# A hybrid decoder block on one core: the mean inside the third product, gates as pairs of 64-row matmuls, one block's residual fetched later, and another end

## The chip, the core and the metric

The kernel runs on one core of one Trainium2 chip. The metric is the device time of one execution in microseconds. The work is on five engines with queues of their own: TensorE (PE, with its weight loads PEld), VectorE (DVE), ScalarE (ACT), GpSimd (POOL) and SyncE (SP), which issues most DMAs.

## What is computed

One decoder layer over 2048 positions of 1024 channels, in fp32. The reference, cut:

```python
h = rms_norm(x, norm1_g)
z = h @ w_in                       # 2*1024 + 3*512 columns
lru_x, lru_gate, sc_b, sc_c, sc_x = split(z)
lru_x = causal_dwconv(lru_x, lru_conv_w) + lru_conv_b
r = sigmoid(blockdiag16x64(lru_x, wa) + ba)     # 16 heads of 64 channels
i = sigmoid(blockdiag16x64(lru_x, wx) + bx)
log_a = -8 * r * softplus(-lam)
hs = scan(a = exp(log_a), b = sqrt(1 - exp(2*log_a)) * i * lru_x)
y = concat(hs * gelu(lru_gate), sc_b * causal_dwconv(sc_c * sc_x))
x = x + y @ w_out
h = rms_norm(x, norm2_g)
gate, up = split(causal_dwconv(h @ w_up, ffn_conv_w))
x = x + (gelu(gate) * up) @ w_down
out = rms_norm(x, final_g)
```

## The kernel before

Channels lie on the 128 partitions, positions in the free dimension. The sequence goes in two halves of T = 1024 positions, each in two blocks of NB = 512. Every fp32 product is made of three matmuls in fp32r: each operand is split into a high and a low part (`split`: ACT makes the high part, DVE the low one), and high x high, high x low and low x high are summed in PSUM.

Six phases follow each other: the input phase of the first half (7 to 345 us), its output sweep o0 (to 461), the input phase of the second half (to 789), sweep o1 (to 910), then up and down of the first half and of the second. A sweep multiplies by w_out or w_down in seven passes over 512 x 512 blocks and adds the residual (`sweeps`, `TAKEN`). The residual blocks "11", "12", "22" and "21" are fetched at steps of the sweep that a table gives.

In the input phase (`in_phase`) one product of 48 matmuls (8 blocks of channels x 3 x 2 blocks of positions) makes 128 columns of z. Products 0 and 8 come first, each step as x arrives. Then comes the mean: the squares of x are summed on ACT and DVE into ss_a, split into rh_a and rl_a (`mean_split`), and four matmuls with a matrix of 1/D sum them over the partitions into ms_a; ACT and DVE make the inverse root of it (`inv_rms`), by which each product is scaled when it leaves PSUM. In the first half product 1 stands before the four matmuls. Then twelve units run in the order L0 L1 S0 L2 L3 S1 L4 L5 L6 L7 S2 S3. An L unit c is a group of 128 recurrent channels, two heads: xl (product c, scaled), cv (the convolution: one step on ACT, three on DVE), xch and xcl (its high and low parts), the gates, sigmoids r and i, then a, m (in the tile of cv), a scan and the product with the gelu of the gate g (product 8 + c).

The gates of a unit are one group of 12 matmuls, three for each of r and i and each block, with the 128 x 128 weights of r and of i (two heads on the diagonal, zeros beside it) in gw, the split of a raw tile that is loaded behind the weights of product 8 + c. "Gate group c" below is the group of unit c. On PE it stands behind the product of the next unit and ahead of product 8 + c + 1.

PE, SP and POOL run in the order in which the program issues their instructions; for ACT and DVE a scheduler sets the order, with priorities (HP 120, HW 90, HE 30). Raw weights have two buffers (wr), PSUM has eight banks of 128 x 512, and a product or a gate tile of both blocks takes two.

`decay_rates` computes 8 * softplus(-lam) from the parameters with some thirty operations of 128 x 8. `sum_step` makes sums of w_out blocks in DRAM (so_d), a copy on SP's queue and an adding DMA on POOL's after each product, once the list `ready` allows it. At the end, `down1_done` squares the last block of the output (sq_last), splits the square and adds it to the last mean, and `finish_block` scales eight blocks and sends them out.

Of the kernel before, what the change touches and what calls it, by code (L numbers as in the profile page):

```python
# [7 lines left out]
F32 = mybir.dt.float32  # L8
# [4 lines left out]
P = 128  # L13
# [13 lines left out]
HE = 30  # L27
WARM = 11
NOUT = NLRU + NSC
NI = NFF // 2  # L30
# [38 lines left out]
def block_kernel(  # L69
# [28 lines left out]
    nc8 = cp.tile([P, NLRU], F32, name="nc8")  # L98
    xl_halo = cp.tile([P, NLRU, 3], F32, name="xl_halo")
    h_last = cp.tile([P, NLRU], F32, name="h_last")  # L100
    p_halo = cp.tile([P, NSC, 2], F32, name="p_halo")
# [47 lines left out]

    def decay_rates():  # L150
        z = cp.tile([P, NLRU], F32, name="dz")
        t = cp.tile([P, NLRU], F32, name="dt")
        e = cp.tile([P, NLRU], F32, name="de")
        s2 = cp.tile([P, NLRU], F32, name="ds2")
        lam = prm[:, O_LAM : O_LAM + NLRU]
        nc.vector.tensor_scalar(z, lam, -1.0, None, ALU.mult)
        nc.vector.tensor_tensor(z, z, lam, ALU.max)
        nc.scalar.activation(t, z, AF.Tanh, scale=1.0 / 16.0)
        nc.vector.tensor_scalar(e, t, 1.0, None, ALU.add)
        nc.vector.reciprocal(e, e)  # L160
        nc.vector.tensor_scalar(t, t, -1.0, 1.0, ALU.mult, ALU.add)
        nc.vector.tensor_tensor(e, e, t, ALU.mult)
        for _ in range(3):
            nc.vector.tensor_tensor(e, e, e, ALU.mult)
        nc.vector.tensor_scalar(t, e, 2.0, None, ALU.add)
        nc.vector.reciprocal(t, t)
        nc.vector.tensor_tensor(t, t, e, ALU.mult)
        nc.vector.tensor_tensor(s2, t, t, ALU.mult)
        nc.vector.tensor_scalar(e, s2, 1.0 / 21.0, None, ALU.mult)
        for k in range(9, 0, -1):  # L170
            nc.vector.scalar_tensor_tensor(e, e, 1.0 / (2 * k + 1), s2, ALU.add, ALU.mult)
        nc.vector.scalar_tensor_tensor(e, e, 1.0, t, ALU.add, ALU.mult)
        nc.vector.tensor_scalar(t, lam, -1.0, 0.0, ALU.mult, ALU.max)
        nc.vector.scalar_tensor_tensor(t, e, 2.0, t, ALU.mult, ALU.add)
        nc.vector.tensor_scalar(c8, t, 8.0, None, ALU.mult)
        nc.vector.tensor_scalar(nc8, t, -8.0, None, ALU.mult)
# [25 lines left out]

    gate_raw = {}

    def load_parts(src, name, parts, gate=None):
# [5 lines left out]
        for i in range(parts):  # L211
            ks = slice(i * n, (i + 1) * n)
            nc.sync.dma_start(raw[:, ks], src[:, ks])
            with tc.high_priority(offset=HW):
                split(hi[:, ks], lo[:, ks], raw[:, ks])
            if gate is not None and i == 0:
                gate_raw[gate] = tile_[:, 4, : 2 * P]
                nc.sync.dma_start(gate_raw[gate], w_gate[gate])
            yield hi, lo
# [17 lines left out]

    def product(ps, wts, acts):
        n = len(acts)
        for k in range(n):  # L240
            product_step(ps, wcol(wts, k), acts[k], k == 0, k == n - 1)

# [16 lines left out]
    def inv_rms(acc, name, parts=None):  # L259
# [3 lines left out]
        for i, x in enumerate(terms):  # L263
            for b, p in enumerate(pss):
                nc.tensor.matmul(p, ones_r, r32(x[:, blk(b)]), start=i == 0, stop=i == len(terms) - 1)
        with tc.high_priority(offset=HP):
# [46 lines left out]
    def gate_weights(c, half):  # L313
        raw = gate_raw[c]
        gw = flat(act(f"gw{half}_{c}"))
        hi, lo = gw[:, 0 : 2 * P], gw[:, 2 * P : 4 * P]
        with tc.high_priority(offset=HW):
            split(hi, lo, raw)
        return hi, lo

    def lru_gates(c, half, xc, gw):
        pss = []
        for g, name in enumerate("ri"):
            ps = pst2(f"z{name}{half}_{c}")
            product_step(ps, wcol(gw, g), xc, True, True)
            pss.append(ps)
        return pss

    def lru_scan(c, half, cv, g, ps_r, ps_i):
        n = f"{half}_{c}"  # L330
        r, i, a = (flat(act(f"{x}{n}")) for x in "ria")
        with tc.high_priority(offset=HP):
            for dst, ps, o in ((r, ps_r, O_BA), (i, ps_i, O_BX)):
                for b, p in enumerate(ps):
                    nc.scalar.activation(dst[:, blk(b)], p, AF.Sigmoid, bias=col(o + c))
        nc.vector.tensor_tensor(i, i, cv, ALU.mult)
# [23 lines left out]

    def in_product(o, half, acts):
        ps = pst2(f"zin{half}_{o}")
        product(ps, load_weights(w_in[o], f"in{half}_{o}", o - NLRU if NLRU <= o < 2 * NLRU else None), acts)
        if len(ready) > half:
# [47 lines left out]
    def in_phase(half, acts, acc, between):  # L412
# [18 lines left out]
        parts = mean_split(acc, f"a{half}")  # L431
        gw = gate_weights(0, half)
        ps_2 = in_product(1, half, acts) if half == 0 else None
        rs = inv_rms(acc, f"a{half}", parts)
        nc.gpsimd.tensor_copy(ones[:, 0:1], rs[:, 0:1])
        ready.append(True)
        xc, cv = lru_conv(0, half, pss[0], rs)
        if half == 0:
            decay_rates()
        cur = (xc, cv, lru_gate(0, half, pss[1], rs))  # L440
        ps_n = None
        for n, (kind, c) in enumerate(UNITS):
            nxt = UNITS[n + 1] if n + 1 < len(UNITS) else None
            if kind == "L":
# [5 lines left out]
                ps_g = in_product(NLRU + nxt[1], half, acts) if n == 0 else None  # L450
                if n > 0:
                    gw = gate_weights(c, half)
                gates = lru_gates(c, half, xc, gw)
                if nxt[0] == "L":
# [226 lines left out]
    def sweeps(half, wsrc, fsrc, ni, name, residual, done, beside, tail=0):  # L681
        res = {}
        fetch = {}
        for key, at in (("11", ((0, 1), (0, 2))), ("12", ((1, 0), (1, 0))), ("22", ((1, 1), (1, 2))), ("21", ((6, 1), (6, 1)))):
            for p, a in enumerate(at):
                fetch.setdefault(a, []).append((key, p))
        step = 0
        for s, (wo, fo, on_x) in enumerate(SWEEPS):
# [40 lines left out]
            for m in range(4):  # L729
                for h in held:  # L730
                    mm((m,), *h)
                for key, sign, final in TAKEN[s]:
                    r = res[key][m // 2][:, m % 2, :]
                    with tc.high_priority(offset=HP if last else HE):
                        nc.vector.tensor_tensor(r, r, ps[m], ALU.add if sign > 0 else ALU.subtract)
# [160 lines left out]
    def finish_block(t, rs):  # L896
        for key in ("12", "22") if t else ("11", "21"):
            mh = PLACE[key][0]
            for p, r in enumerate(kept[key]):
                for m in range(2):  # L900
                    scaled(r[:, m, :], 4 * mh + 2 * p + m, rs)
                c = 4 * mh + 2 * p
                o = T + t * NB
                defer(4, yT[c : c + 2, :, o : o + NB].rearrange("m p c -> p m c"), r)

    def down1_done(key, m, r):
# [3 lines left out]
        with tc.high_priority(offset=HP if key == "21" else 0):  # L910
            if key == "21" and m == 3:
                sq = flat(tmp("sq_last"))[:, :NB]
                nc.scalar.activation(sq, r[:, 1, :], AF.Square)
                terms.extend(mean_split(sq, "l2"))
                return
# [33 lines left out]
def _arrange(i):  # L949
# [6 lines left out]
    out["w_in"] = f["w_in"][0].reshape(KC, P, 28, P).transpose(2, 1, 0, 3).reshape(28, P, D)  # L956
    wg = np.zeros((NLRU, P, 2, P), x.dtype)
    for g, name in enumerate(("lru_wa", "lru_wx")):
        w = f[name][0].reshape(NLRU, 2, 64, 64)
        wg[:, 0:64, g, 0:64] = w[:, 0]  # L960
        wg[:, 64:128, g, 64:128] = w[:, 1]
    out["w_gate"] = wg.reshape(NLRU, P, 2 * P)
    w = f["w_out"][0].reshape(NOUT, P, D)
# [42 lines left out]
```

## Time and profile before

| | us |
|---|---|
| median of 3 runs (2302.47 to 2308.16) | 2305.39 |
| profiled execution | 2304.75 |
| its span in the trace | 2302.9 |
| PE busy | 2272.7 |
| DVE busy | 1723.8 |
| ACT busy | 1136.0 |
| POOL busy | 141.4 |

The time of the profiled execution is 1.85 us longer than its span, which ends with the last instruction's effect. A matmul's record is longer than the interval to the next one's start, since matmuls follow each other in the array before the first is through; so two starts are compared where the price of one is wanted.

### The profile page before, as it was taken

How to read it: one execution, taken by the hardware profiler on the slowest of the kernel's cores; microseconds unless marked ns; L12 is line 12 of the kernel's file. 1: busy time of each engine (PE TensorE's matmuls, PEld its weight loads, DVE VectorE, ACT ScalarE, POOL GpSimd, SP SyncE). 2: the span in 40 equal slices, each digit the busy share in tenths (PEclk: the TensorE clock that was granted, in tenths of full speed). 3: DMA queues.
4: the chain of work that ended last, by engine and by line, in shares of the span. 5: the costliest groups of instructions: out<-in, count | busy, mean ns of one | idle time of the engine just before them, and what ended most of it. 6: DMA issues, size and time to landing. Idle time of an engine off the chain costs nothing.

```text
span 2302.9 us, 26017 instructions
## 1 busy us (share of the span) xinstructions
PE 2272.7 (99%) x9984; PEld 1875.2 (81%) x9984; DVE 1723.8 (75%) x1910; ACT 1136.0 (49%) x1242; POOL 141.4 (6%) x232
## 2 busy tenths in 40 slices
PE   8999999999999999999999999999999999999997
PEld 7788887888888878888888888888888888888885
DVE  7656668767666898888787877578888888886556
ACT  5553645545547345554444444455544444443443
POOL 0001000000010000111010100000010000000000
PEclk9999999999999999999999999999999999999999
DMA  5356257766755767223232348576223232348754
GB/s 182 106 141 162 80 183 243 271 177 147 195 156 143 235 246 248 102 92 114 92 114 92 114 155 289 204 242 216 87 92 115 92 119 88 122 169 324 256 186 181
DMA packets 145597, 378.28 MB, mean 164 GB/s; under 512 B 13824, under 2 KB 17024, under 8 KB 144896
## 3 DMA queue, kind: packets, MB, share of 16 engines
q1 hardware_dynamic: 135680, 357.74, 44.8%
q0 software_dynamic: 9792, 18.88, 5.2%
q8 instruction: 78, 1.28, 0.2%
q14 instruction: 47, 0.39, 0.0%
HBM read 289.53 MB, written 124.78 MB: 180 GB/s over the span
## 4 chain that ended last, share of the span: by engine, by line
PE 94%; DVE 3%; DMA 1%; ACT 1%; issue 1%; SPq 0%; DVEq 0%; ACTq 0%
PE zin_b L234 25%; PE zx L581 23%; PE zc L581 11%; PE dx L700 11%; PE dy L700 8%; PE za L581 6%; PE ox L700 5%; PE oy L700 3%; PE zr_b L234 1%; PE zi_b L234 1%; DMA x<-in_xT 1%; DMA wr_d<-sd_d_S 0%; DVE x2r L879 0%; DVE cv L294 0%; DVE fl_o L196 0%
## 5 line engine op out<-in xcount | busy, mean ns | idle before, releaser
L234 PE MATMUL zin_b<-xh,wh_in 128*128 128x512 f32 x896 | 277.2, 390 | 4.8 <-DVE ss_a L270 2.6
L234 PE MATMUL zin_b<-xl,wh_in 128*128 128x512 f32 x896 | 277.0, 390 | 0.1
L234 PE MATMUL zin_b<-xh,wl_in 128*128 128x512 f32 x896 | 276.3, 390 | 0.0
L234 PEld LDWEIGHTS zin_b<-xh,wh_in 128*128 128x128 f32 x896 | 168.5, 188 | 40.9 <-DVE ss_a L270 3.5
L234 PEld LDWEIGHTS zin_b<-xl,wh_in 128*128 128x128 f32 x896 | 168.5, 188 | 36.4 <-DVE xl L402 1.7
L234 PEld LDWEIGHTS zin_b<-xh,wl_in 128*128 128x128 f32 x896 | 168.5, 188 | 35.0
L196 DVE TENSOR_TENSOR fl_d<-wr_d,fh_d 128x1024 fp32r<-128x1024 f32 x84 | 102.8, 1223 | 104.5 <-ACT fh_d L195 102.2
L195 ACT ACTIVATE fh_d<-wr_d 128x1024 fp32r<-128x1024 f32 x84 | 89.1, 1061 | 176.7 <-PE dy L700 79.7
L196 DVE TENSOR_TENSOR wla_up<-wr_up,wha_up 128x1024 fp32r<-128x1024 f32 x48 | 58.8, 1226 | 139.0 <-ACT wha_up L195 139.0
L700 PE MATMUL dx<-fl_d,wh_d 128*128 128x512 f32 x384 | 149.5, 389 | 0.8 <-DVE fl_d L196 0.8
L700 PE MATMUL dx<-fh_d,wl_d 128*128 128x512 f32 x384 | 149.4, 389 | 0.0
L700 PE MATMUL dx<-fh_d,wh_d 128*128 128x512 f32 x384 | 149.4, 389 | 0.0
L557 DVE TENSOR_TENSOR wr_up<-wr_up 128x512 f32<-128x512 f32 x192 | 130.0, 686 | 14.7 <-DMA wr_up<-in_w_up 13.5
L195 ACT ACTIVATE wh_in<-wr_in 128x1024 fp32r<-128x1024 f32 (+1 forms) x62 | 60.2, 973 | 159.1 <-DMA wr_in<-in_w_in 154.4
L196 DVE TENSOR_TENSOR wl_in<-wr_in,wh_in 128x1024 fp32r<-128x1024 f32 (+1 forms) x62 | 69.1, 1118 | 80.4 <-ACT wh_in L195 80.4
L581 PE MATMUL zc<-hhB,whd_up 128*128 128x512 f32 x384 | 126.0, 389 | 0.0
L294 DVE SCALAR_TENSOR_TENSOR cu<-un,prm,cu 128x1024 f32<-128x1024 f32 x96 | 122.7, 1278 | 4.3 <-ACT cu L290 4.3
L196 DVE TENSOR_TENSOR wl_d<-wr_d,wh_d 128x1024 fp32r<-128x1024 f32 x84 | 102.5, 1220 | 28.0 <-ACT wh_d L195 25.6
L294 DVE SCALAR_TENSOR_TENSOR cg<-ug,prm,cg 128x1024 f32<-128x1024 f32 x96 | 122.8, 1279 | 0.4
L581 PE MATMUL zx<-ht,whc_up 128*128 128x512 f32 x384 | 118.2, 389 | 0.0
L592 ACT ACTIVATE ug<-zx 128x512 f32<-128x512 f32 x96 | 57.5, 599 | 122.8 <-PE zx L581 122.6
L195 ACT ACTIVATE wh_d<-wr_d 128x1024 fp32r<-128x1024 f32 x84 | 88.4, 1053 | 59.8 <-DMA wr_d<-sd_d_S 32.0
(258 smaller groups left out, 5590.2 us busy)
## 6 DMA issues: line engine op xcount, KB each, us to landing
wr_up<-in_w_up SPq DMA_DIRECT2D x96, 512.0 KB, 4.9
wr_in<-in_w_in SPq DMA_DIRECT2D x54, 512.0 KB, 4.1
wr_d<-sd_d_S SPq DMA_DIRECT2D x48, 512.0 KB, 3.7
wr_d<-f_d_T SPq DMA_DIRECT2D x48, 512.0 KB, 4.9
f_d_B<-cu SPq DMA_DIRECT2D x72, 256.0 KB, 2.4
wr_d<-in_w_down SPq DMA_DIRECT2D x36, 512.0 KB, 3.6
wr_d<-f_d_B SPq DMA_DIRECT2D x36, 512.0 KB, 4.6
wr_o<-so_d_S SPq DMA_DIRECT2D x24, 512.0 KB, 4.5
```

The source lines that it names most:

```text
L195: nc.scalar.activation(r32(hi), src, AF.Copy)
L196: nc.vector.tensor_tensor(r32(lo), src, hi, ALU.subtract)
L234: nc.tensor.matmul(ps[t], r32(a), r32(b[:, blk(t)]), start=(first and i == 0), stop=(last and i == 2))
L294: nc.vector.scalar_tensor_tensor(dst, src[:, k : k + T], col(o_w + k), dst, ALU.mult, ALU.add)
L557: nc.vector.tensor_tensor(raw[:, o, :], raw[:, a, :], raw[:, b, :], ALU.add)
L581: nc.tensor.matmul(ps, r32(p[:, s]), r32(self.hs[k][x][o]), start=f and i == 0, stop=l and i == 2, skip_group_check=True,)
L592: nc.scalar.activation(dst, self.x, AF.Copy)
L700: nc.tensor.matmul(ps[m], r32(p), r32(x[:, k, :]), start=first and i == 0 and n == 0, stop=(last or not on_x) and i == ni - 1 and n == 2, ...
```

## The change

- The mean of the first half is computed inside product 1, after two of its eight steps (`mid`), where it stood behind it. The marker that keeps POOL from starting the sums before the mean is written into dz, and `decay_rates`, which works on dz, so comes after the mean. `ready` is set one product earlier.
- Gates: the weights of both gates come as one 128 x 128 tile: rows 0 to 63 hold head 0's r and i columns, rows 64 to 127 head 1's i and r columns. A group is again 12 matmuls, but of 64 rows, in six pairs: one on the upper and one on the lower row half, into different banks. r and i of the two heads then lie on different partition halves of the banks, so each sigmoid becomes two of 64 partitions. The weights are split right behind the load of their product (in the program's order).
- Residuals: block "22" is fetched at the step where "12" was, and "12" at the two steps where "22" was.
- End: the last square goes to the mean as it is, by one fp32 matmul with `ones`, where it was split for two fp32r matmuls; the outputs of `finish_block` go out in eight DMAs of one 128 x 512 block, where they went in four of two; the last residual addition has a higher priority.

```diff
 WARM = 11
+HALVES = (slice(0, P // 2), slice(P // 2, P))
 NOUT = NLRU + NSC
...
     xl_halo = cp.tile([P, NLRU, 3], F32, name="xl_halo")
+    dz = cp.tile([P, NLRU], F32, name="dz")
+    mark = dz[:, 0:1]
     h_last = cp.tile([P, NLRU], F32, name="h_last")
...

-    def decay_rates():
-        z = cp.tile([P, NLRU], F32, name="dz")
+    def decay_rates(z):
         t = cp.tile([P, NLRU], F32, name="dt")
...
     gate_raw = {}
+    gate_w = {}

...
             if gate is not None and i == 0:
-                gate_raw[gate] = tile_[:, 4, : 2 * P]
+                gate_raw[gate] = tile_[:, 4, :P]
                 nc.sync.dma_start(gate_raw[gate], w_gate[gate])
...

-    def product(ps, wts, acts):
+    def product(ps, wts, acts, mid=None):
         n = len(acts)
         for k in range(n):
+            if mid is not None and k == 2:
+                mid()
             product_step(ps, wcol(wts, k), acts[k], k == 0, k == n - 1)
...
             for b, p in enumerate(pss):
-                nc.tensor.matmul(p, ones_r, r32(x[:, blk(b)]), start=i == 0, stop=i == len(terms) - 1)
+                w, v = (ones_r, r32(x[:, blk(b)])) if i < 2 else (ones, x[:, blk(b)])
+                nc.tensor.matmul(p, w, v, start=i == 0, stop=i == len(terms) - 1)
         with tc.high_priority(offset=HP):
...
     def gate_weights(c, half):
-        raw = gate_raw[c]
         gw = flat(act(f"gw{half}_{c}"))
-        hi, lo = gw[:, 0 : 2 * P], gw[:, 2 * P : 4 * P]
+        hi, lo = gw[:, :P], gw[:, P : 2 * P]
         with tc.high_priority(offset=HW):
-            split(hi, lo, raw)
+            split(hi, lo, gate_raw[c])
         return hi, lo

     def lru_gates(c, half, xc, gw):
-        pss = []
-        for g, name in enumerate("ri"):
-            ps = pst2(f"z{name}{half}_{c}")
-            product_step(ps, wcol(gw, g), xc, True, True)
-            pss.append(ps)
+        pss = [pst2(f"z{name}{half}_{c}") for name in "ri"]
+        for i, (a, b) in enumerate(((gw[0], xc[0]), (gw[0], xc[1]), (gw[1], xc[0]))):
+            for t in range(T // NB):
+                for ps, rows in zip(pss, HALVES):
+                    nc.tensor.matmul(ps[t], r32(a[rows, :]), r32(b[rows, blk(t)]), start=i == 0, stop=i == 2)
         return pss

-    def lru_scan(c, half, cv, g, ps_r, ps_i):
+    def lru_scan(c, half, cv, g, ps_a, ps_b):
         n = f"{half}_{c}"
         r, i, a = (flat(act(f"{x}{n}")) for x in "ria")
         with tc.high_priority(offset=HP):
-            for dst, ps, o in ((r, ps_r, O_BA), (i, ps_i, O_BX)):
-                for b, p in enumerate(ps):
-                    nc.scalar.activation(dst[:, blk(b)], p, AF.Sigmoid, bias=col(o + c))
+            for dst, o, order in ((r, O_BA, (0, 1)), (i, O_BX, (1, 0))):
+                for rows, ps, k in zip(HALVES, (ps_a, ps_b), order):
+                    for b, p in enumerate(ps):
+                        nc.scalar.activation(
+                            dst[rows, blk(b)], p[HALVES[k], :], AF.Sigmoid, bias=prm[rows, o + c : o + c + 1]
+                        )
         nc.vector.tensor_tensor(i, i, cv, ALU.mult)
...

-    def in_product(o, half, acts):
+    def in_product(o, half, acts, mid=None):
         ps = pst2(f"zin{half}_{o}")
-        product(ps, load_weights(w_in[o], f"in{half}_{o}", o - NLRU if NLRU <= o < 2 * NLRU else None), acts)
+        c = o - NLRU if NLRU <= o < 2 * NLRU else None
+        wts = load_weights(w_in[o], f"in{half}_{o}", c)
+        if c is not None:
+            gate_w[c] = gate_weights(c, half)
+        product(ps, wts, acts, mid)
         if len(ready) > half:
...
         parts = mean_split(acc, f"a{half}")
-        gw = gate_weights(0, half)
-        ps_2 = in_product(1, half, acts) if half == 0 else None
-        rs = inv_rms(acc, f"a{half}", parts)
-        nc.gpsimd.tensor_copy(ones[:, 0:1], rs[:, 0:1])
-        ready.append(True)
+        rss = []
+
+        def mean():
+            rss.append(inv_rms(acc, f"a{half}", parts))
+            nc.gpsimd.tensor_copy(mark, rss[0][:, 0:1])
+            ready.append(True)
+
+        if half == 0:
+            gate_w[0] = gate_weights(0, half)
+            ps_2 = in_product(1, half, acts, mean)
+        else:
+            ps_2 = None
+            mean()
+        rs = rss[0]
         xc, cv = lru_conv(0, half, pss[0], rs)
         if half == 0:
-            decay_rates()
+            decay_rates(dz)
         cur = (xc, cv, lru_gate(0, half, pss[1], rs))
...
                 ps_g = in_product(NLRU + nxt[1], half, acts) if n == 0 else None
-                if n > 0:
-                    gw = gate_weights(c, half)
-                gates = lru_gates(c, half, xc, gw)
+                gates = lru_gates(c, half, xc, gate_w[c])
                 if nxt[0] == "L":
...
         fetch = {}
-        for key, at in (("11", ((0, 1), (0, 2))), ("12", ((1, 0), (1, 0))), ("22", ((1, 1), (1, 2))), ("21", ((6, 1), (6, 1)))):
+        for key, at in (("11", ((0, 1), (0, 2))), ("22", ((1, 0), (1, 0))), ("12", ((1, 1), (1, 2))), ("21", ((6, 1), (6, 1)))):
             for p, a in enumerate(at):
...
                     r = res[key][m // 2][:, m % 2, :]
-                    with tc.high_priority(offset=HP if last else HE):
+                    with tc.high_priority(offset=HE if not last else 2 * HP if m == 3 else HP):
                         nc.vector.tensor_tensor(r, r, ps[m], ALU.add if sign > 0 else ALU.subtract)
...
                 for m in range(2):
-                    scaled(r[:, m, :], 4 * mh + 2 * p + m, rs)
-                c = 4 * mh + 2 * p
-                o = T + t * NB
-                defer(4, yT[c : c + 2, :, o : o + NB].rearrange("m p c -> p m c"), r)
+                    c = 4 * mh + 2 * p + m
+                    scaled(r[:, m, :], c, rs)
+                    defer(4, yT[c, :, T + t * NB : T + (t + 1) * NB], r[:, m, :])

...
                 nc.scalar.activation(sq, r[:, 1, :], AF.Square)
-                terms.extend(mean_split(sq, "l2"))
+                terms.append(sq)
                 return
...
     out["w_in"] = f["w_in"][0].reshape(KC, P, 28, P).transpose(2, 1, 0, 3).reshape(28, P, D)
-    wg = np.zeros((NLRU, P, 2, P), x.dtype)
-    for g, name in enumerate(("lru_wa", "lru_wx")):
-        w = f[name][0].reshape(NLRU, 2, 64, 64)
-        wg[:, 0:64, g, 0:64] = w[:, 0]
-        wg[:, 64:128, g, 64:128] = w[:, 1]
-    out["w_gate"] = wg.reshape(NLRU, P, 2 * P)
+    w = [f[name][0].reshape(NLRU, 2, 64, 64) for name in ("lru_wa", "lru_wx")]
+    out["w_gate"] = np.concatenate(
+        [np.concatenate([w[k][:, k], w[1 - k][:, k]], axis=2) for k in range(2)], axis=1
+    )
     w = f["w_out"][0].reshape(NOUT, P, D)
```

On PE in the first input phase the mean stands behind product 1 (zin_1, 48 matmuls, the last two of them here; zin_9 is the next product) before:

```order
L234 MATMUL zin_1_b_483<-xh_7_437,wl_in_1_487 128x512
L234 MATMUL zin_1_b_484<-xh_7_437,wl_in_1_487 128x512
L265 MATMUL ms_a_0_539<-rh_a_476,ones_r 128x512
L265 MATMUL ms_a_512_540<-rh_a_476,ones_r 128x512
L265 MATMUL ms_a_0_539<-rl_a_477,ones_r 128x512
L265 MATMUL ms_a_512_540<-rl_a_477,ones_r 128x512
L234 MATMUL zin_9_b_603<-xh_0_290,wh_in_9_606 128x512
```

After, it stands inside product 1, behind its twelfth matmul; zin_1 goes on behind it:

```order
L237 MATMUL zin_1_b_484<-xh_1_318,wl_in_1_488 128x512
L237 MATMUL zin_1_b_485<-xh_1_318,wl_in_1_488 128x512
L271 MATMUL ms_a_0_504<-rh_a_477,ones_r 128x512
L271 MATMUL ms_a_512_505<-rh_a_477,ones_r 128x512
L271 MATMUL ms_a_0_504<-rl_a_478,ones_r 128x512
L271 MATMUL ms_a_512_505<-rl_a_478,ones_r 128x512
L237 MATMUL zin_1_b_484<-xh_2_342,wh_in_1_487 128x512
```

The four ms_a matmuls moved up by 36 rows. In the input phase further on, this is gate group 5 on PE before (zr and zi: the banks of r and i):

```order
L234 MATMUL zr_5_b_1865<-xch_5_1724,gw_5_1862 128x512
L234 MATMUL zr_5_b_1866<-xch_5_1724,gw_5_1862 128x512
L234 MATMUL zr_5_b_1865<-xcl_5_1725,gw_5_1862 128x512
L234 MATMUL zr_5_b_1866<-xcl_5_1725,gw_5_1862 128x512
L234 MATMUL zr_5_b_1865<-xch_5_1724,gw_5_1862 128x512
L234 MATMUL zr_5_b_1866<-xch_5_1724,gw_5_1862 128x512
L234 MATMUL zi_5_b_1873<-xch_5_1724,gw_5_1862 128x512
```

And after, at the same place; zr holds the upper row half's results, zi the lower one's:

```order
L331 MATMUL zr_5_b_1885<-xch_5_1740,gw_5_1775 128x512
L331 MATMUL zi_5_b_1887<-xch_5_1740,gw_5_1775 128x512
L331 MATMUL zr_5_b_1886<-xch_5_1740,gw_5_1775 128x512
L331 MATMUL zi_5_b_1888<-xch_5_1740,gw_5_1775 128x512
L331 MATMUL zr_5_b_1885<-xcl_5_1741,gw_5_1775 128x512
L331 MATMUL zi_5_b_1887<-xcl_5_1741,gw_5_1775 128x512
L331 MATMUL zr_5_b_1886<-xcl_5_1741,gw_5_1775 128x512
```

The number of matmuls is the same, and the two banks alternate from one matmul to the next. On ACT between xch_5 and xch_6, from the first sigmoid of unit 4 to gw_5, the gate weights of unit 5 (a_4 and cv_4 are steps of unit 4), before:

```order
L335 ACTIVATE r_4_1728<-zr_4_b_1698,prm 128x512
L335 ACTIVATE r_4_1728<-zr_4_b_1699,prm 128x512
L335 ACTIVATE i_4_1729<-zi_4_b_1706,prm 128x512
L335 ACTIVATE i_4_1729<-zi_4_b_1707,prm 128x512
L338 ACT_TABLE_LOAD
L338 ACTIVATE a_4_1730<-r_4_1728,nc_80 128x1024
L339 ACTIVATE cv_4_1561<-r_4_1728,c_79 128x1024
L195 ACTIVATE gw_5_1862<-wr_in_13_1748 128x256
```

After:

```order
L341 ACTIVATE r_4_1744<-zr_4_b_1714,prm 64x512
L341 ACTIVATE r_4_1744<-zr_4_b_1715,prm 64x512
L341 ACTIVATE r_4_1744<-zi_4_b_1716,prm 64x512
L341 ACTIVATE r_4_1744<-zi_4_b_1717,prm 64x512
L341 ACTIVATE i_4_1745<-zr_4_b_1714,prm 64x512
L341 ACTIVATE i_4_1745<-zr_4_b_1715,prm 64x512
L341 ACTIVATE i_4_1745<-zi_4_b_1716,prm 64x512
L341 ACTIVATE i_4_1745<-zi_4_b_1717,prm 64x512
L346 ACT_TABLE_LOAD
L346 ACTIVATE a_4_1746<-r_4_1744,nc_80 128x1024
L197 ACTIVATE gw_5_1775<-wr_in_13_1768 128x128
L347 ACTIVATE cv_4_1578<-r_4_1744,c_79 128x1024
```

Eight sigmoids stand where four stood, and gw_5 has moved from behind cv_4 to ahead of it. Gate group 7's weights, gw_7, stood ahead of cv_6 before and do so after.

## Rows read from the trace of the kernel before

**Rows 1.** The page's part 1: busy time, share of the span and instructions of each engine.

```profile
PE 2272.7 (99%) x9984; PEld 1875.2 (81%) x9984; DVE 1723.8 (75%) x1910; ACT 1136.0 (49%) x1242; POOL 141.4 (6%) x232
```

**Rows 2.** The waits of PE over the whole span: who waited, for whom, then the total in us, the times and the longest.

```profile
PE oy L700 <- DVE fl_o L196: 3.9, 3, 1.6
PE zin_b L234 <- DVE ss_a L270: 2.6, 1, 2.6
```

**Rows 3.** The timeline of PE in the first 80 us: start, duration (both us; of the whole pair where x2), line, operation, out<-in, shape, count, and in brackets the idle time before with its releaser.

```profile
12.40 0.62 PE L234 MATMUL zin_b<-xh,wh_in 128*128 128x512 f32 x2
13.08 0.73 PE L234 MATMUL zin_b<-xl,wh_in 128*128 128x512 f32 x2
...
43.70 0.61 PE L265 MATMUL ms_a<-rl_a,ones_r 128*128 128x512 f32 x2
46.95 1.09 PE L234 MATMUL zin_b<-xh,wh_in 128*128 128x512 f32 x2 [2.64 <-DVE ss_a L270]
47.88 0.63 PE L234 MATMUL zin_b<-xl,wh_in 128*128 128x512 f32 x2
...
59.82 0.73 PE L234 MATMUL zr_b<-xch,gw 128*128 128x512 f32 x2 [1.34 <-ACT xch L195]
61.08 0.74 PE L234 MATMUL zr_b<-xcl,gw 128*128 128x512 f32 x2 [0.53 <-DVE xcl L196]
...
75.79 0.73 PE L234 MATMUL zr_b<-xch,gw 128*128 128x512 f32 x2 [1.23 <-ACT gw L195]
```

**Rows 4.** The timeline of DVE in the first 31 us, same columns (L176 is the last of the decay rates, rl_a the low half of the first mean's sum).

```profile
11.68 0.16 DVE L176 TENSOR_SCALAR nc<-dt 128x8 f32<-128x8 f32 x1
11.75 1.28 DVE L402 SCALAR_TENSOR_TENSOR xl<-x,prm,xh 128x1024 fp32r<-128x1024 f32 x1
...
30.89 1.21 DVE L196 TENSOR_TENSOR rl_a<-ss_a,rh_a 128x1024 fp32r<-128x1024 f32 x1
```

**Rows 5.** The view of one tile, zr_b: operation, count, then min/median/max of the duration in ns.

```profile
L234 PEld LDWEIGHTS zr_b<-xch,gw x64: 186/188/189, 59.8 to 733.6; 128*128 128x128 f32 x64
L234 PE MATMUL zr_b<-xch,gw x64: 389/389/504, 59.8 to 733.8; 128*128 128x512 f32 x64
...
L335 ACT ACTIVATE r<-zr_b,prm x32: 677/686/692, 70.5 to 741.6; 128x512 f32<-128x512 f32 x32
```

**Rows 6.** The timeline of PE at gate group 5 of the first half and gate group 7 of the second.

```profile
239.12 0.62 PE L234 MATMUL zr_b<-xch,gw 128*128 128x512 f32 x2
...
732.66 0.61 PE L234 MATMUL zr_b<-xch,gw 128*128 128x512 f32 x2
```

**Rows 7.** Windows of the first half: the stretch, its length, and the busy time of PE, PEld, DVE, ACT and POOL with instructions in brackets, then the granted clock, the DMA share and GB/s. This one lies between the starts of gate groups 6 and 7.

```profile
263.60:288.08 24.48, 24.48 (x109) 20.28 (x108) 17.66 (x18) 13.76 (x16) 0.80 (x3) 1.00 0.35 111
```

**Rows 8.** The timeline of ACT from 217 to 290 us, around gate groups 5 to 7 of the first half.

```profile
218.34 1.06 ACT L195 ACTIVATE wh_in<-wr_in 128x1024 fp32r<-128x1024 f32 x1 [5.19 <-DMA wr_in<-in_w_in]
224.60 1.06 ACT L195 ACTIVATE xch<-cv 128x1024 fp32r<-128x1024 f32 x1 [4.06 <-DVE cv L294]
...
226.97 1.27 ACT L335 ACTIVATE r<-zr_b,prm 128x512 f32<-128x512 f32 x2
...
229.42 1.28 ACT L338 ACT_TABLE_LOAD   x1
...
231.77 1.14 ACT L339 ACTIVATE cv<-r,c 128x1024 f32<-128x1024 f32 x1
232.81 0.40 ACT L195 ACTIVATE gw<-wr_in 128x256 fp32r<-128x256 f32 x1
...
251.88 1.06 ACT L195 ACTIVATE xch<-cv 128x1024 fp32r<-128x1024 f32 x1 [4.32 <-DVE cv L294]
...
279.95 1.06 ACT L195 ACTIVATE xch<-cv 128x1024 fp32r<-128x1024 f32 x1 [5.22 <-DVE cv L294]
...
287.12 0.40 ACT L195 ACTIVATE gw<-wr_in 128x256 fp32r<-128x256 f32 x1
```

**Rows 9.** The timeline of DVE around the same groups, and at gate group 7 of the second half.

```profile
214.62 1.29 DVE L371 TENSOR_TENSOR xl<-zin_b,ss_a 128x512 f32<-128x512 f32 x2 [0.21 <-PE zin_b L234]
...
233.24 0.42 DVE L196 TENSOR_TENSOR gw<-wr_in,gw 128x256 fp32r<-128x256 f32 x1 [1.39 <-ACT gw L195]
...
260.51 0.43 DVE L196 TENSOR_TENSOR gw<-wr_in,gw 128x256 fp32r<-128x256 f32 x1 [1.39 <-ACT gw L195]
...
287.55 0.42 DVE L196 TENSOR_TENSOR gw<-wr_in,gw 128x256 fp32r<-128x256 f32 x1 [1.54 <-ACT gw L195]
...
732.03 0.43 DVE L196 TENSOR_TENSOR gw<-wr_in,gw 128x256 fp32r<-128x256 f32 x1 [1.54 <-ACT gw L195]
```

**Rows 10.** The chain that ended last, in order of time, from 2270 us: start, us, what.

```profile
2288.61 0.64 ACT rh_l L195
...
2290.55 0.70 ACT ry_l L269
```

**Rows 11.** The timeline of PE at the start: the warm-up.

```profile
1.00 4.54 PE L746 MATMUL warm<-ones 128*128 128x128 f32 x22 [1.00 <-POOL eps L96]
```

**Rows 12.** The timeline of SP from 2285 us: the issues of the last outputs.

```profile
2294.89 4.35 SPq L192 DMA_DIRECT2D out_yT<-x2r  x4
```

**Rows 13.** The page's part 6: DMA issues with count, KB each and median us from issue to landing.

```profile
wr_in<-in_w_in SPq DMA_DIRECT2D x54, 512.0 KB, 4.1
...
f_d_B<-cu SPq DMA_DIRECT2D x72, 256.0 KB, 2.4
```

## The prediction

> **What bounds the kernel now.** I read busy time first: TensorE is busy 2272.7 of 2302.9 us [rows 1], so the time is the number of matmuls times their interval, plus some 30 us of gaps and ends. From the start of gate group 6 to that of gate group 7 there are 108 matmuls (two products of 48 and 12 of gates) in 24.48 us with TensorE busy throughout [rows 7]: 226.7 ns each. That is the price of a matmul taken away where TensorE never waits. Next I read who made it wait: each entry is small, the largest being the sweeps o0 and o1 (oy, 3.9 us together) and the first product after the mean (2.6) [rows 2], then the first two gate groups (1.34 and 0.53, 1.23) [rows 3]. Then, for the gates, I read ACT and DVE beside them [rows 6, 8, 9], because a faster TensorE reaches the point at which those two are late next. They are nearly late already: the split weights of gate group 7 are ready at 287.55 + 0.42 = 287.97 us [rows 9] and TensorE takes them at 288.08, where the window of [rows 7] ends. In the second half it is 732.46 against 732.66 [rows 6, 9].
>
> **The change, part by part.** The sum is made against the profiled run, 2304.75 us, which is 0.64 below the median of 2305.39.
>
> *Mean inside the third product.* The four ms_a matmuls stand behind 12 matmuls of zin_1 where they stood behind 48: 36 x 226.7 ns = 8.2 us earlier, at about 35.1 us. Their inputs are done by 30.89 + 1.21 = 32.1 [rows 4], so no new wait starts there. Now ms_a starts its second pair at 43.70, and zin_9 starts at 46.95 [rows 3]. Without a gap it would come at 43.70 + 2 x 0.227 = 44.15, and its first pair then runs at a longer interval (0.93 from 46.95 to 47.88 for 0.45): 2.8 + 0.5 = 3.3 us, all gone, because what it waits for moves 8 us and TensorE only 3. The gates of unit 0 lose the 1.34 and 0.53 of idle [rows 3] and about 0.4 of slow restarts, 2.3 together: ACT and DVE get their 8 us of lead, of which a weight load that now stands ahead of xch_0 on ACT takes some. Gates of unit 1 wait 1.23 for their weights [rows 3], which now come early; but the banks of zr_0 and zi_0 come free only after eight sigmoids, which is late by an estimated 0.6 to 1.6, so I count nothing there. Sum **-5.6**, bounds -7.1 and -3.3.
>
> *Decay rates.* They leave the start, where the second x tile's residue (xl) is only begun at 11.75, right behind them [rows 4]; from 12.40 to 13.08 a pair of matmuls takes 0.68 for 0.45 [rows 3], and with two smaller waits after it I take **-0.5**. The tiny DVE operations go between the conv steps after the mean, where the 8 us of lead cover them; without that cover some 30 of them at 0.16 [rows 4] would cost 5 us.
>
> *The gates on TensorE.* 16 groups of 12 matmuls cost 12 x 226.7 = 2.72 us each. The twelve new ones have 64 rows and come in six pairs on different row halves and banks. No pair of that kind is in the trace, so I bound it. If two run at once, a group takes six intervals: -1.36. If every weight load keeps its 188 ns [rows 5] and no two overlap, a pair takes 376 in place of 453: -0.46. If nothing overlaps: 0. If each change between full and half rows also waits for the array to empty, a group pays up to twice 389 - 227 + 188 = 0.35 us: +0.7. Today loads of 188 hide under intervals of 227, so the engine does overlap loading and multiplying; I take **1.25 saved per group**, near the end of full overlap.
>
> The Trainium skill ("TensorE: Matmul & The Clock Gate", Part 3) says that matmuls in different row groups run at once and gives 3.07 for four tiles of 32 rows; by that share of the ideal, a pair of 64 rows would run 1.5 times as fast and a group would save about 0.9. The Trainium skill ("TensorEngine Tiling (Array Packing)", Key Properties) also says that a change of the tiling mode drains the engine, which speaks against groups of only twelve; no row here shows either.
>
> *The gates on ACT.* The sigmoids read 512 columns in 0.69 us each [rows 5], four of them in 2.45 us, from 226.97 to the table load at 229.42 [rows 8]. With 64 rows per instruction there are eight, and each still streams 512 columns: I count 8 x 0.6 = 4.8, so **+2.4 us per unit** (bounds 0 and +2.4). ACT is half idle [rows 1], so that costs nothing where it has slack, but between units 4 and 7 it stands in a chain. There, xch follows xch by 27.28 us (224.60, 251.88) and 28.07 (279.95) [rows 8], while TensorE needs 24.48 [rows 7]: TensorE catches up with the chain, which it does only just not reach. Worked out from the end of xch_5 at 225.66:
> - gw_5 and gw_6 stand behind the eight sigmoids (+2.4) but are moved ahead of cv (1.04 between 231.77 and 232.81 [rows 8]) and are half as wide (-0.25 over both engines): +1.1. gw_7 stood ahead of cv before: +2.15.
> - xch_6 and xch_7 come later too: cv of the next unit is now behind the scan on DVE. I add the durations of the rows in the new order and get 28.2 per unit: +0.9 for xch_6, +0.1 more for xch_7 (bounds 0 and 4.8 for both).
> - Slack now: group 5: 239.12 - 233.66 = 5.46; group 6: 263.60 - 260.94 = 2.66; group 7: 0.11 [rows 6, 7, 9].
> - With TensorE 1.25 earlier per group: group 5: 5.46 - 1.25 - 1.1 = 3.1, no wait. Group 6: 2.66 - 2.5 - 2.0 = -1.8, a wait. Group 7: 0.11 - 3.75 - 3.15 = -6.8, of which 1.8 was waited before, so **5.0 us of wait in front of gate group 7**.
>
> So of 8 x 1.25 = 10 us per half, 6.8 are given back: **-3.2 per half, -6.4 in all**. That takes it that xch_5 itself moves forward with TensorE (its xl starts 0.21 after the product ends at 214.62 [rows 9]). If it stays (the weight split at 218.34 waited 5.19 for a DMA [rows 8]), up to 5 us more per half are lost.
>
> *Fetch order of residuals.* Same sizes; in sweep o1 the operations on DVE keep their order, so most of oy's 3.9 us of waits [rows 2] stays: 0, bounds -2 and +1.
>
> *Sums so_d one product earlier.* SP copies and POOL adds start where both have nothing due: 0, cover being the idle queues; +1 if they delay a weight load at the start.
>
> *End.* From rh_l at 2288.61 to ry_l at 2290.55 are 1.94 us [rows 10]; now one fp32 matmul does it. The warm-up's 11 fp32 matmuls make 22 records in 4.54 us on 128 columns [rows 11], so 512 columns cost between two plain intervals with a tail (0.6) and 2 x 4 x 0.206 = 1.65; I take 1.0, since the warm-up is the program's first work: 1.94 - 1.0, about -1.0. The last output goes in 256 KB for 512 KB, and the issue at its end leaves 2302.9 - (2294.89 + 4.35) = 3.7 us to the end of the span [rows 12]; DMAs of such sizes land in 2.4 and 4.1 [rows 13]. I take -0.8, as four earlier transfers share the queue (bounds -0.2 and -1.5). Sum **-1.8**.
>
> Total: -5.6 - 0.5 - 6.4 - 1.8 = -14.3, which gives 2290.5.
>
> **The rivals.** *The chain doesn't hold TensorE back* (gw moves early enough, or xch_6 and xch_7 come sooner because cv now precedes the weight splits that wait for DMA). For it: DVE waits for ACT and ACT for DMA in that stretch, so there is air to squeeze. Against it: 0.11 us of slack and 2.4 us more of sigmoids. Then the gates give 20: 2304.75 - 7.9 - 20 = 2277.
>
> *The pairs do not overlap.* TensorE arrives as before and gw_7 comes 3.15 - 0.11 = 3.0 late per half: 2304.75 - 7.9 + 6.1 = 2303; with 0.46 per group saved by shorter pairs, a half saves 8 x 0.46 = 3.7 and waits 3.0 + 3 x 0.46 = 4.4: 2298.
>
> *Slower: the switches between full and half rows cost.* At 0.7 us per group without overlap, a half pays 8 x 0.7 = 5.6 and still waits 3.0 - 3 x 0.7 = 0.9 at gate group 7: 2304.75 - 7.9 + 13 = 2310, and more if the mean gives less. This decides from about 0.3 us per group. The steady 226.7 across the change from zin_b to zr_b today says nothing, as both are full matmuls.
>
> **How the numbers follow.** Forecast 0.47 (2285 to 2297), free chain 0.20, no overlap 0.20, switches 0.13. A difference within 0.3% (2298.5 to 2312.3) is about what a measurement of this kernel can't tell from none. Faster: 0.47 + 0.20 + 0.08 of the third = 0.75; slower 0.07, the worse half of the fourth; same 0.18. The range 2275 to 2306 leaves out the lower end of the free chain and most of the switches.
>
> **What would show it.** No wait at zin_9 and at gate group 0; gate groups of about 1.45 us for 2.72; eight sigmoids in 4.8 us; waits before gate groups 6 and 7, in both halves, released by ACT or DVE gw, of about 2 and 5 us; ms_l to ry_l about 1 us shorter. It is wrong if gate groups take 2.7 us or more, or if group 7 doesn't wait.

## The result, and the profile after

The changed kernel takes 2315.40 us (median of 6 runs) beside 2304.61 for the kernel before: 1.0044 times as long, 95% interval 1.0031 to 1.0057. That is some 10.8 us slower; the forecast was 2290.5 us, 14.3 below the profiled run before.

The waits of PE over the whole span, after (who waited, for whom; total us, times, longest):

```profile
PE zr_b L331 <- ACT gw L197: 22.4, 7, 5.5
PE oy L719 <- DVE fl_o L198: 3.9, 3, 1.6
PE zin_b L237 <- ACT xh L413: 2.6, 1, 2.6
...
PE zr_b L331 <- DVE xcl L198: 0.3, 1, 0.3
```

Beside [rows 2] the wait after the mean is gone, and so are those of the first two gate groups [rows 3]. In their place stand seven waits for gate weights, 22.4 us. They are at gate groups 2, 3, 5, 6, 7 of the first half and 6, 7 of the second. The timeline of PE, after, shows a gate group without a wait (668.17, group 4 of the second half) and one behind a wait (299.13, group 7 of the first):

```profile
299.13 0.79 PE L331 MATMUL zr_b<-xch,gw 64*128 64x512 f32 x1 [3.59 <-ACT gw L197]
299.14 0.79 PE L331 MATMUL zi_b<-xch,gw 64*128 64x512 f32 x1
299.73 0.62 PE L331 MATMUL zr_b<-xch,gw 64*128 64x512 f32 x1
299.73 0.63 PE L331 MATMUL zi_b<-xch,gw 64*128 64x512 f32 x1
300.16 0.62 PE L331 MATMUL zr_b<-xcl,gw 64*128 64x512 f32 x1
...
301.99 1.22 PE L237 MATMUL zin_b<-xh,wh_in 128*128 128x512 f32 x2
...
668.17 0.49 PE L331 MATMUL zr_b<-xch,gw 64*128 64x512 f32 x1
668.17 0.49 PE L331 MATMUL zi_b<-xch,gw 64*128 64x512 f32 x1
668.50 0.39 PE L331 MATMUL zr_b<-xch,gw 64*128 64x512 f32 x1
668.51 0.39 PE L331 MATMUL zi_b<-xch,gw 64*128 64x512 f32 x1
668.74 0.39 PE L331 MATMUL zr_b<-xcl,gw 64*128 64x512 f32 x1
...
669.76 0.73 PE L237 MATMUL zin_b<-xh,wh_in 128*128 128x512 f32 x2
```

Two matmuls of a pair start within 0.01 us: the pairs do run at once. The twelve take 1.59 us (668.17 to 669.76) for 2.72. Behind the wait the same twelve take 2.86 (299.13 to 301.99). The windows around that group say why (length; busy time of PE, PEld, DVE, ACT, POOL; then the granted clock, the DMA share and GB/s):

```profile
299.13:301.99 2.86, 2.85 (x12) 1.81 (x13) 1.77 (x3) 2.86 (x3) 0.00 (x0) 0.50 0.49 150
301.99:304.29 2.30, 2.30 (x7) 1.82 (x6) 1.47 (x2) 2.27 (x3) 0.00 (x0) 0.50 0.13 48
304.29:310.00 5.71, 5.71 (x26) 4.73 (x25) 0.64 (x1) 5.63 (x7) 0.00 (x0) 0.98 0.00 0
```

After 3.59 us without work the granted clock is 0.50, the lower of the two levels, until 304.29: here the wait costs more than its idle time.

What the weights wait for is on ACT. Its timeline after, between xch_5 and gate group 7, to read beside [rows 8]:

```profile
231.91 1.06 ACT L197 ACTIVATE xch<-cv 128x1024 fp32r<-128x1024 f32 x1 [4.06 <-DVE cv L300]
...
234.28 1.26 ACT L341 ACTIVATE r<-zr_b,prm 64x512 f32<-64x512 f32 x2
235.55 1.26 ACT L341 ACTIVATE r<-zi_b,prm 64x512 f32<-64x512 f32 x2
236.84 1.26 ACT L341 ACTIVATE i<-zr_b,prm 64x512 f32<-64x512 f32 x2
238.11 1.25 ACT L341 ACTIVATE i<-zi_b,prm 64x512 f32<-64x512 f32 x2
...
241.73 0.29 ACT L197 ACTIVATE gw<-wr_in 128x128 fp32r<-128x128 f32 x1
...
260.32 1.06 ACT L197 ACTIVATE xch<-cv 128x1024 fp32r<-128x1024 f32 x1 [1.09 <-DVE cv L300]
...
288.97 1.06 ACT L197 ACTIVATE xch<-cv 128x1024 fp32r<-128x1024 f32 x1 [4.20 <-DVE cv L300]
```

Eight sigmoids take 5.1 us (234.28 to 238.11 + 1.25) for 2.45, xch follows xch by 28.4 and 28.65 us (forecast 28.2), and gw_5 starts 8.8 us behind the end of xch_5, where it started 7.15 behind it in [rows 8] (the forecast had + 2.4 - 1.04). All that was about as worked out. But xch_5 itself stands at 231.91: 7.3 us later than in [rows 8], where the forecast moved it forward with TensorE, some 11 us by its own terms (5.6 + 0.5 + 4 x 1.25).

A loop leads from the sigmoids of one unit to the xch of a later one by several links; the runs below cut two of them. The first is a buffer: the split gate weights free a raw buffer for which the next weights wait. The end of gw_4's split in the timeline of DVE, after:

```profile
212.50 0.28 DVE L198 TENSOR_TENSOR gw<-wr_in,gw 128x128 fp32r<-128x128 f32 x1
```

The issue of the next weights right behind it, in the timeline of SP, after:

```profile
212.81 6.16 SPq L216 DMA_DIRECT2D wr_in<-in_w_in  x2
```

ACT's split of the second of these loads, and the xl of unit 5 behind DVE's part of that split (timelines of ACT and DVE, after):

```profile
222.99 1.06 ACT L197 ACTIVATE wh_in<-wr_in 128x1024 fp32r<-128x1024 f32 x1 [5.64 <-DMA wr_in<-in_w_in]
...
225.23 1.28 DVE L383 TENSOR_TENSOR xl<-zin_b,ss_a 128x512 f32<-128x512 f32 x2
```

In [rows 8, 9] that split stands at 218.34, with xl ahead of it at 214.62. So what set the start of xch_5 was these weights: they are 4.65 us later, and xl behind their split makes the other 2.6.

The second link is POOL's queue: it clears the halo of the next but one unit's xl only behind the copy of a unit's last state, which waits for the scan (timeline of POOL, after):

```profile
253.68 1.03 POOL L356 COPY h_last<-r 128x1 f32<-128x1 f32 x1 [26.92 <-DVE r L354]
254.65 0.10 POOL L284 MEMSET xl<- 128x3 f32 x1
```

It binds first at unit 2. There the memset stands behind the adding DMAs of the sums, and these behind the copies of the last states (h_last) of units 0 and 1, at 90.39 and 96.16; the convolution waits for it (timelines of POOL and DVE, after):

```profile
117.53 0.90 POOL L367 DMA_DIRECT2D so_d_S<-in_w_out  x1 [10.04 <-issue]
118.10 0.45 POOL L284 MEMSET xl<- 128x3 f32 x1
...
118.58 1.29 DVE L300 SCALAR_TENSOR_TENSOR cv<-xl,prm,cv 128x1024 f32<-128x1024 f32 x1 [11.39 <-POOL xl L284]
```

In the kernel before, this memset stood at 120.10: it moved 2.0 us forward, while gate group 1 on TensorE moved 8.6. With four sigmoids it stands at 114.45 (run 1 below) and 113.50 (run 2), and group 2 does not wait there.

The end, after, in the chain of waits, beside [rows 10]:

```profile
2297.72 0.64 ACT sq_last L931
2298.36 0.04 issue
2298.40 1.14 PE ms_l L271 x2
2299.54 0.02 issue
2299.56 0.70 ACT ry_l L275
```

The fp32 matmul takes 1.14 us in two records.

### The profile page after: what moved, and what is told of

It reads as the page before. It is cut to its first block, busy times and chain, and to the rows that moved or that the text cites. A ratio compares the mean times of both kernels' runs of the same rounds, so it can differ in the third digit from the quotient of the medians.

```text
span 2311.5 us, 26115 instructions
## 1 busy us (share of the span) xinstructions
PE 2266.5 (98%) x9984; PEld 1861.5 (81%) x9984; DVE 1718.1 (74%) x1909; ACT 1179.7 (51%) x1308; POOL 140.3 (6%) x232
## 4 chain that ended last, share of the span: by engine, by line
PE 68%; DVE 9%; ACT 7%; DMA 4%; issue 2%; SPq 0%; POOL 0%; DVEq 0%; ACTq 0%; POOLq 0%
PE zx L600 23%; PE zc L600 11%; PE dx L719 9%; PE dy L719 8%; PE za L600 6%; PE zin_b L237 5%; PE ox L719 4%; PE oy L719 2%; DMA wr_in<-in_w_in 2%; DVE cv L300 1%; ACT i L341 1%; ACT r L341 1%; DVE wl_in L198 1%; DMA wr_d<-f_d_T 1%; DVE r L354 1%
## 5 line engine op out<-in xcount | busy, mean ns | idle before, releaser
L237 PE MATMUL zin_b<-xh,wh_in 128*128 128x512 f32 x896 | 282.0, 396 | 2.6 <-ACT xh L413 2.6
L237 PEld LDWEIGHTS zin_b<-xh,wh_in 128*128 128x128 f32 x896 | 169.1, 190 | 45.2 <-issue 6.0
L576 DVE TENSOR_TENSOR wr_up<-wr_up 128x512 f32<-128x512 f32 x192 | 129.8, 685 | 12.0 <-DMA wr_up<-in_w_up 10.8
```

Of the source, the lines that this page charges most:

```text
L237: nc.tensor.matmul(ps[t], r32(a), r32(b[:, blk(t)]), start=(first and i == 0), stop=(last and i == 2))
L576: nc.vector.tensor_tensor(raw[:, o, :], raw[:, a, :], raw[:, b, :], ALU.add)
```

## Experiments

The kernel before ran beside them on the same chip (medians 2306.22, 2306.24 and 2305.04 us in the three groups of four). Ratios are to it, with 95% intervals.

**1. Gates and sigmoids as before, all else changed.** The diff of the change without its parts on gate_weights, lru_gates, lru_scan and w_gate.

> The changed kernel with the gates, their weights and the four sigmoids as before; the mean, the decay rates, the fetch order and the end stay changed. Theory A (eight sigmoids in the chain gate weights - raw buffer - weights - convolution - xch - sigmoids - next gate weights make TensorE wait): the loss goes, 2297 to 2303 us; 2297 if the chain follows TensorE's earlier start, 2303 if it doesn't and gate groups 6 and 7 wait. Rival C (the 64-row pairs themselves cost, by switches of the tile shape and a lower clock): 2297. Rival D (the loss lies in the mean's new place, the fetch order or the end): about 2315 as in the changed kernel.

2301.68 us, 0.9984 (0.9974 to 0.9993). The loss lies in the gates. The mean's gain shows up to gate group 5 (232.34, 6.8 us earlier than in [rows 6]), and then groups 6 and 7 wait 3.1 us for gate weights in three waits: the gain runs into the chain that had 0.1 us of slack.

**2. Four sigmoids of 128 partitions.**

```diff
-            for dst, o, order in ((r, O_BA, (0, 1)), (i, O_BX, (1, 0))):
...
+            for dst, ps, o in ((r, ps_a, O_BA), (i, ps_b, O_BX)):
+                for b, p in enumerate(ps):
+                    nc.scalar.activation(dst[:, blk(b)], p, AF.Sigmoid, bias=col(o + c))
```

> The changed kernel with four sigmoids of 128 partitions in place of eight of 64: r is read from the banks of the upper row half and i from those of the lower one, so r and i of every second head are exchanged and the output is not the reference's; the amount of all other work is the same. Theory A (length of the sigmoids): gate weights come about 2.6 us earlier per unit and the waits for them fall from 22.4 us to under 6: about 2290. Theory B (the place of the gate weights' split in ACT's order, not the sigmoids' length): waits stay above 12 us and the time above 2303. Rival C (pairs cost by themselves): 2312 or more.

2301.79 us, 0.9981 (0.9971 to 0.9991): 13.6 us below the changed kernel, but the waits for gate weights are still 15.0 us. The length of the sigmoids is a large part, and the place of the split another. It also equals run 1, which has the old gates and the split at its old place: as long as that chain binds, 16 shorter gate groups bring nothing that shows.

**3. The gate weights in another pool.**

```diff
-        gw = flat(act(f"gw{half}_{c}"))
+        gw = flat(wpage(f"gw{half}_{c}"))
```

> The changed kernel with one word changed: the split gate weights take a buffer of the weights' pool in place of one of the 28 pages that also hold r, i, a and xch; their split then stands ahead of the sigmoids in ACT's order. Theories A and B: the gate weights no longer wait behind sigmoids and no longer hold a raw buffer, the waits for them go to nearly 0 and so does the lower clock behind the waits: 2279 to 2285 us. Rival C (pairs cost by themselves): still above 2305.

2293.85 us, 0.9945 (0.9930 to 0.9961): 21.5 us below the changed kernel by one word. No wait for gate weights is left, so the pairs cost nothing by themselves. It missed its 2279 to 2285 by waits of another kind, both in the first half, at gate groups 2 and 7 (waits of PE in this run):

```profile
PE zr_b L331 <- ACT xch L197: 4.4, 1, 4.4
PE zr_b L331 <- ACT i L341: 4.1, 1, 4.1
```

**4. Only the eight sigmoids, in the kernel before.**

```diff
-                for b, p in enumerate(ps):
-                    nc.scalar.activation(dst[:, blk(b)], p, AF.Sigmoid, bias=col(o + c))
+                for rows in (slice(0, P // 2), slice(P // 2, P)):
+                    for b, p in enumerate(ps):
+                        nc.scalar.activation(
+                            dst[rows, blk(b)], p[rows, :], AF.Sigmoid, bias=prm[rows, o + c : o + c + 1]
+                        )
```

> The kernel before with one thing changed: each of the four sigmoids of a unit is split into two of 64 partitions. Theory A: gate group 7, which has 0.1 us of slack, and then 3 and 6 wait; 2309 to 2320 us. Theory B (the place alone, which is the old one here) and rival C: 2304 to 2306, as ACT is half idle.

2322.66 us, 1.0073 (1.0052 to 1.0093): 16.4 us slower, beyond theory A's upper end, with 14.0 us in seven waits for gate weights, from gate group 1 of the first half on. Splitting instructions on an engine that is half idle costs more than the whole change lost.

**5. Run 4 with the gate weights in the weights' pool** (the diff of run 3).

> The kernel before with eight sigmoids of 64 partitions per unit (as in the run that cost 16.8 us), and the split gate weights in a buffer of the weights' pool. Theory 1 (the sigmoids' length counts because the gate weights' split stands behind them and holds a raw buffer): most of the 16.8 us goes, 2304 to 2309 us. Theory 2 (the length counts wherever that split stands, by xch and by the banks that the sigmoids free): 2314 or more.

2308.17 us, 1.0012 (1.0003 to 1.0022): 14.5 of the 16.4 us are gone, as theory 1 has it.

**6. The gate weights in the temporaries' pool** (`tmp` for `act`).

> The changed kernel with the split gate weights in a page of the temporaries' pool: for some units, not all, their split then stands ahead of the sigmoids in ACT's order, and the weights' pool is left alone. Theory 1: groups 2, 4, 5 and 7 don't wait for gate weights, 3 and 6 do: 2290 to 2302 us. Theory 2: 2305 or more.

2340.16 us, 1.0152 (1.0136 to 1.0168). Theory 1 had the groups right and the time wrong; theory 2's open range holds the time, though not by the sigmoids' length alone. Groups 3 and 6 of both halves now wait up to 13.3 us, 45.2 in all: there the split stands still later in ACT's order, behind the unit's last ACT step. Which pool gives the page decides the place, in either direction. A page freed in the pool of 28 is not what helped in run 3, for this run frees it too.

**7. Four sigmoids and the weights' pool** (diffs of runs 2 and 3).

> The changed kernel with four sigmoids (r and i of every second head exchanged, so not the reference's output) and the split gate weights in the weights' pool. Both causes of late gate weights are out, so all of TensorE's gain should show: 2304.6 - 6.8 (mean, as seen up to gate group 4) - 15 (gates) - 1.2 (end) = 2281.6; theory 1 gives 2280 to 2288, at most 8 us below the 2293.9 with eight sigmoids; theory 2 gives more than 12 below it. If a cost of the pairs on TensorE beside the waits was overlooked: 2290 or more.

2278.58 us, 0.9886 (0.9871 to 0.9902), a little below the range, with no wait at a gate group. It is 15.3 us below run 3, so theory 2 was right that the sigmoids' length still counted there. Run 5 had spoken for theory 1; neither was the whole.

**8. Run 1 with the weights' pool.**

> The changed kernel with the gates, their weights' shape and the four sigmoids as before, and the split gate weights in the weights' pool. If the mean's gain of about 6.8 us was given back at gate groups 6 and 7 only because their weights are late, it is kept now: 2295 to 2298 us. If something else gives it back: 2300 to 2303 as without the change of pool.

2293.55 us, 0.9952 (0.9936 to 0.9967), better than expected: the mean's gain is kept once the gate weights are early. Run 7, with the pairs in place of these gates, is 15.0 us below it: about what 16 groups of 12 matmuls save at 0.91 us each (14.6).

**9. Run 3 with h_last on DVE.** The remaining wait of run 3 at group 7 was traced back to POOL: there the convolution of unit 7 waited for the memset behind h_last (copy at 272.59, memset at 272.71).

```diff
-            nc.gpsimd.tensor_copy(h_last[:, c : c + 1], h[:, T - 1 : T])
+            nc.vector.tensor_copy(h_last[:, c : c + 1], h[:, T - 1 : T])
```

> The changed kernel with the gate weights in the weights' pool (2293.9 us) and the copy of a unit's last state (h_last) on DVE in place of POOL. Theory 3: what makes the sigmoids' length count there is POOL's queue in the first half: the clearing of the next-but-one unit's halo (xl) stands behind the copy of h_last, which waits for sigmoids, a and scan, so the convolution waits for the scan; with the copy gone from POOL the wait before gate group 7 (4.1 us and the low clock behind it) goes, the one before group 2 (4.4 us, behind an adding DMA on POOL) stays: 2285 to 2289 us. Theory 2 (the sigmoids' length on ACT itself): 2292 or more.

2279.80 us, 0.9898 (0.9881 to 0.9914). Both waits went, that of group 2 too, so the range was too high: two copies of h_last stood on POOL ahead of the adding DMA that I had made answerable. The largest waits of PE in this run:

```profile
PE oy L719 <- DVE fl_o L198: 3.5, 3, 1.6
PE zin_b L237 <- ACT xh L413: 1.8, 2, 1.3
```

And two of its windows, between the starts of gate groups 5, 6 and 7 (columns as above):

```profile
227.25:250.82 23.57, 23.57 (x110) 18.99 (x110) 15.73 (x17) 15.93 (x19) 1.18 (x2) 1.00 0.21 68
250.82:274.39 23.57, 23.57 (x109) 18.99 (x109) 17.27 (x18) 17.19 (x20) 1.15 (x2) 1.00 0.27 92
```

No gate group waits, with eight sigmoids, and a unit takes 23.57 us for the 24.48 of [rows 7]. Unlike runs 2 and 7 this version exchanges nothing, and it beats both kernels: 25 us under the one before, 36 under the changed one.

**10. Run 9 with the halos' memset on DVE too** (`nc.vector.memset` in with_halo).

> As the run with h_last on DVE, and the clearing of the halos on DVE too, so that no convolution waits for POOL. Theory 3: the waits before gate groups 2 and 7 both go, and with all gains kept: 2278 to 2283 us, close to the 2278.6 with four sigmoids. Theory 2: 2290 or more.

2280.83 us, 0.9898 (0.9883 to 0.9913): no different from run 9, so the copy was the link.

**11. h_last and memset on DVE, gate weights where the change has them.**

> The changed kernel with h_last and the halos' clearing on DVE, and the gate weights left in the pages where the change has them. If POOL's queue is the larger link of the loop: waits for gate weights fall from 22.4 us to under 10, 2290 to 2300 us. If the gate weights behind the sigmoids with their raw buffer are enough to close the loop: 2308 to 2316 us.

2299.25 us, 0.9975 (0.9965 to 0.9985): the waits for gate weights fall from 22.4 to 11.7 us (in the profiled execution, 2294.75 us, the fastest of eight). The time is inside the first range, the waits a little above it: POOL's queue is one link, and the gate weights' place alone keeps the other half of the waits.

**12. Run 5 with h_last and memset on DVE.**

> The kernel before with eight sigmoids, the gate weights in the weights' pool, and h_last and the halos' clearing on DVE. Theory 3: both links are cut, so eight sigmoids cost nothing: 2300 to 2304 us, at or below the kernel before. Theory 2: 2308 as without the change of queue.

2301.48 us, 0.9984 (0.9975 to 0.9994). Eight sigmoids per unit then cost nothing beside the kernel before, where they cost 16.4 us with both links closed. What these cuts bring the kernel before with its four sigmoids was not run.

## Why the prediction was wrong, step by step

- **Mean and decay rates: right.** Gate group 0 starts at 54.46, 5.4 us earlier than in [rows 3], and ends 7.5 us earlier (56.05 for 63.51); without the 1.1 that the pairs save in it, that is 6.3 for 6.1 forecast. No wait is left at zin_9. The wait of gate group 1, left out of the sum, went too: 6.8 in run 1.
- **The gates on TensorE: right in kind, too large.** A unit gets 0.91 us shorter for 1.25. Six pairs save 1.36, and the first intervals around a change of shape are 0.32 to 0.33 us in place of 0.23, some 0.2 us per change. The Trainium skill ("TensorEngine Tiling (Array Packing)", Key Properties) says that a change of the tiling mode drains the engine; these 0.2 us agree with it, though no run shows what the engine does in them. They did not decide.
- **The eight sigmoids: right.** +2.6 us per unit for 2.4, period 28.4 for 28.2.
- **The step that failed: "xch_5 itself moves forward with TensorE".** It moved 7.3 us back. I had read its start from one row, the xl that follows a product by 0.21 us, though the weights' split, at 218.34 in [rows 8], set it. The case against it was put at 5 us per half without a chance of its own; that leaves out the mean, with which it is 11 in the first half. And the table of slack began at unit 5, as if the turns before it cost nothing. But in the first half unit 2's convolution waited for POOL's queue, so xch_2 came 2.3 us earlier (123.56 for 125.86) and xch_3 0.5 (146.38 for 146.84), TensorE 8.6. Gate group 2 stands behind xch_2 and its weights, and gate group 3 behind weights that follow xch_3 and the eight sigmoids of unit 2. So groups 2, 3 and 5, which the sum left without a wait, waited 1.6, 5.5 and 3.6 us, 10.7 together.
- **Waits at groups 6 and 7: right in size, in part by luck.** They are 6.8 us in the first half, as forecast, and 5.3 in the second, 12.1 for 13.6. But xch_5 had not moved forward in the second half either (2.0 us later, counted from that half's gate group 0), and in the first half TensorE had lost its lead at groups 2, 3 and 5.
- **The lower clock behind a wait was left out.** At the start of gate group 1 TensorE was 8.6 us ahead of before, at the end 8.6 behind: 17.2 us were lost. In the same stretch 15 shorter groups saved 13.7, and the sweep and the parts behind it another 4.6 (o1 -2.4, the phases up to the end -1.0, the end -1.2). So 35.5 us were lost to the waits: 22.7 as idle time at gate groups, and the rest, 12.8 by that difference, as restarts and half-speed matmuls behind them. Counted from group to group against run 9, the six stretches up to gate group 7 of the second half that begin with such a wait hold some 13 us beyond the idle time, too.
- **Fetch order: right at 0.** Sweep o1, counted from the last matmul ahead of it, lasts 118.3 to 120.6 us in the ten profiles with the new order and 118.7 to 121.3 in the four with the old one. **End: -1.2 for -1.8**: from the last square's end to ry_l 1.20 us for 1.94, and the other 0.5 behind that; in runs with the change it takes 15.5 to 16.0 us from the last dx to the span's end, without it 16.8 to 17.1.
- **The rivals.** The one that ended slower, switches of shape, has the right sign and the wrong cause. The free chain (2277) is what runs 7 and 9 made of the change, within 3 us, once both links were cut or the sigmoids were four.

Not tried: each of mean and end alone; they are read from traces.

## What to carry to other kernels

A loop through an engine that is half idle has a period, and if that lies above the bound engine's, the slack is spent before it shows: work the loop out from its first turn, with every queue and every buffer that it passes, and ask of each link (a page's pool, a tiny copy on a shared queue) whether it must be there. Before a busy engine is given less work, look for who arrives only just in time; here moving one tile to another pool and one 128 x 1 copy to another engine was worth 36 us, and the shorter matmuls without them nothing (runs 1 and 2).

## What the runs showed of the hardware

- Two 64-row matmuls on different row halves start within 0.01 us of each other and cost one interval, 0.227 us the pair; a change between full and half rows cost some 0.1 us at each of its two sides.
- A sigmoid of 64 x 512 takes as long as one of 128 x 512: 0.63 us apart in the changed kernel, 0.61 before.
- After 3.6 us of idle TensorE the granted clock was 0.50 for 5.2 us (299.13 to 304.29), 12 gate matmuls in it taking 2.86 us for 1.59. After 3.64 us at gate group 5 it fell only inside the group (0.73 in its mean), where pairs start 0.24 us apart at first (242.41 to 242.65) and 0.42 later (243.17 to 243.59).
